# Hybrid block on one core: background steps twice per weight chunk, scores and transposes of p apart

## The chip, the cores and the metric

The kernel runs on one core of one Trainium2 chip. The metric is the device time of one execution in microseconds, median of three runs. The engines have in-order programs of their own: PE (TensorE matmuls and transposes), DVE (VectorE), ACT (ScalarE), POOL (GpSimd) and SP (SyncE, which issues the loads of weights). Accumulators lie in PSUM, everything else in SBUF.

## The reference

One layer on 512 tokens of 1024 features, all in float32. Between two feed-forward parts stands the mixed part, which the change touches:

```
h = rmsnorm(x);  xr, gr, q, k, v, ga, gb = split(h @ w_in)
xc = conv4(xr)                                  # centred, depthwise
a = exp(-8 * r * softplus(-lam));  bx = sqrt(1 - a*a) * (i * xc)   # r, i = sigmoid(gates(xc))
y_lru = (scan_fwd(a, bx) + scan_bwd(a, bx)) * gelu(gr)
q, k = rmsnorm per head of q, k                 # 16 heads of 64
p = softmax(q k^T + bias, over a window of 8 rows x 32 columns)
y_att = p @ v
x = x + (sigmoid(ga) * y_lru + sigmoid(gb) * y_att) @ w_out
```

## The kernel before

Every large product is made in three matmuls of split operands (wh xh + wh xl + wl xh; L147 to L149, and L704 to L706 for q, k, v). A weight chunk is one load of 128 x 1024 floats on SP, one rounding to wh on ACT (L120) and one subtraction to wl on DVE (L123), then 24 matmuls of 512 columns on PE. Three buffers take the raw weights, four each wh and wl. PSUM has four slots named acc and four named aux.

While PE works through the chunks, two background lanes are mixed in. Each is a list of generators: `lru(fs)` for four blocks of the recurrence at a time, and `heads(hf, ...)` for one half of the attention heads (eight of sixteen). `weave(rate)` (L488) adds the rate to what a lane is owed and runs it from one `yield` to the next while a whole step is owed. It is called once behind each chunk. RATE gives the steps per chunk for the phases: xr (the eight chunks of the recurrence's input), t0 (q, k and v of half 0), t1 (q, k, v of half 1) and g (the three gates). Each half's attention is appended when its v group is done, so half 0 runs in t1 and half 1 in g.

The steps of the LRU: gates on PE, ACT and DVE; then per block and direction one exp with a combination (L659), one square root with a product (L664), one scan (L670 forward, L672 backward, with the sum L673).

The steps of attention: rq from the sums of squares (L754 to L756; the sums are L719, the copies out of PSUM L717); the products of q and k with rq (L761); then `start` makes the transposes of q and k for two heads (L770, L772) and splits them (ACT L776, L778, DVE L777 ql, L779 kl); `scores` has 12 matmuls (L796) into two slots, each read by DVE with bias and running maximum (L807, so and nmx), exponentiated on ACT (L810) and normalised on DVE (L812, L816); `turn` transposes p on PE (L824) and copies it out (L827, PT); `apply` multiplies with v (L836) and copies att out (L846). In half 0 a unit is two of four column blocks of a pair of heads, in half 1 all four, with the second pair of slots from acc.

The order of each engine's program is made by a scheduler that respects dependences and priorities, evictions and splits being marked as high priority. So an instruction issued in a step can move ahead of what was written earlier. `after(i, prev)` sets an edge that keeps one instruction behind another in the order on its engine and adds no wait between engines.

Of the kernel before, what the change touches and what calls it, by code (L numbers as in the profile page):

```python
# [16 lines left out]
P = 128  # L17
T = 512
D = 1024
KT = D // P  # L20
# [38 lines left out]
ATT_LAG = (1, 2), (1, 2)  # L59

RATE = {
    "xr": {"lru": 4, "att": 0.0},
    "t0": {"lru": 3, "att": 0.0},
    "t1": {"lru": 2, "att": 0.75},
    "g": {"lru": 3, "att": 0.85},
}


# [1 line left out]
def block_kernel(ctx: ExitStack, tc, a, out):  # L70
# [8 lines left out]
    dram = ctx.enter_context(tc.tile_pool(name="dram", bufs=1, space=bass.MemoryType.DRAM))  # L79

    uid = [0]

    def nm(s):
        uid[0] += 1
# [61 lines left out]
    def mm3(ps, wh, wl, xh, xl, first, last, skip=False):  # L146
        nc.tensor.matmul(ps, wh, xh, start=first, stop=False, skip_group_check=skip)  # L147
        nc.tensor.matmul(ps, wh, xl, start=False, stop=False, skip_group_check=skip)  # L148
        nc.tensor.matmul(ps, wl, xh, start=False, stop=last, skip_group_check=skip)  # L149

    def feat_chunk(src, nk, xh, xl, ps, k0, ktot, act=True):
        H, L = load_w(src, nk * P, act)
        for k in range(nk):
            s = slice(k * P, (k + 1) * P)
            kk = k0 + k
            mm3(ps, H[:, s], L[:, s], xh[kk], xl[kk], kk == 0, kk == ktot - 1)


    def make_xg(gcol, tag):
# [46 lines left out]
    def after(i, prev):  # L206
# [2 lines left out]
        tc.add_manual_dep(i, prev.name, mybir.DependencyInfo(  # L209
            mybir.DependencyClass.NoSync, mybir.DependencyReason.DATA), reason="order")  # L210


    mark = {}

    def sub(out_, in0, in1, neg=False):

# [462 lines left out]
    rb = None  # L679
    for f in range(KT):  # L680
        ps = acc_t()
        feat_chunk(a["wxr"][f], KT, xh, xl, ps, 0, KT)
        if f == 0:
            rb, rcol, vx = rstd(ssum)
            epsv = const.tile([P, NCB], F32, name="epsv")
            nc.vector.tensor_scalar(epsv, vx, EPS, None, ALU.mult)
        conv(f, ps, rb)
        weave(RATE["xr"])
        if (f + 1) % LRU_F == 0:
            lanes["lru"].append(lru(range(f + 1 - LRU_F, f + 1)))  # L690
# [4 lines left out]
    def tok_group(w, hf):  # L695
        pss = [acc_t() for _ in range(NCB)]
        for kp in range(4):
            H, L = load_w(a["wqkv"][w * 2 + hf, kp], 1024)
            for j in range(NCB):
                tj = slice(j * P, (j + 1) * P)  # L700
                for k in range(2):
                    kk = kp * 2 + k
                    s = slice(k * T, (k + 1) * T)
                    nc.tensor.matmul(pss[j], xh[kk][:, tj], H[:, s], start=kk == 0, stop=False)  # L704
                    nc.tensor.matmul(pss[j], xl[kk][:, tj], H[:, s], start=False, stop=False)  # L705
                    nc.tensor.matmul(pss[j], xh[kk][:, tj], L[:, s], start=False, stop=kk == KT - 1)  # L706
            if kp < 3:
                weave(RATE[phase[0]])
        return pss
# [39 lines left out]
    def heads(hf, raws, st):  # L749

        rq = tiny.tile([P, 2, NCB, 8], F32, tag="rq", name=nm("rq"))
        for w in range(2):
            for j in range(NCB):
                nc.vector.tensor_scalar(rq[:, w, j, :], st[:, w, j, :], 1.0 / HD, epsv[:, j : j + 1], ALU.mult, ALU.add)  # L754
        nc.scalar.activation(rq, rq, AF.Sqrt)
        nc.vector.reciprocal(rq, rq)  # L756
        yield
        for w in range(2):
            for j in range(NCB):
                t = raws[w][j].rearrange("p (h d) -> p h d", d=HD)  # L760
                nc.vector.tensor_tensor(t, t, rq[:, w, j, :].unsqueeze(2).to_broadcast([P, 8, HD]), ALU.mult)  # L761
            yield
        qk, rss, soft, PTs = {}, {}, {}, {}

# [1 line left out]
        def start(fi):  # L766
            fs = slice(fi * P, (fi + 1) * P)
            pq, pk = aux_t(), aux_t()
            for j in range(NCB):
                nc.tensor.transpose(pq[:, j * P : (j + 1) * P], raws[0][j][:, fs], ident)  # L770
            for j in range(NCB):
                nc.tensor.transpose(perm(pk)[:, j], raws[1][j][:, fs], ident)  # L772
            rev = lambda t: t.rearrange("p (j t) -> p j t", j=NCB)[:, :, ::-1]
            fwd = lambda t: t.rearrange("p (j t) -> p j t", j=NCB)
            qh, ql, kh, kl = (big_t(F32R, n=n) for n in ("qh", "ql", "kh", "kl"))
            nc.scalar.activation(rev(qh), fwd(pq), AF.Copy, scale=gq8)  # L776
            nc.vector.scalar_tensor_tensor(rev(ql), fwd(pq), gq8, rev(qh.bitcast(F32)), ALU.mult, ALU.subtract)  # L777
            nc.scalar.activation(kh, pk, AF.Copy, scale=gk)  # L778
            nc.vector.scalar_tensor_tensor(kl, pk, gk, kh.bitcast(F32), ALU.mult, ALU.subtract)  # L779
            grid = lambda t: t.rearrange("p (r c) -> p r c", r=ROWS)  # L780
            qk[fi] = qh, ql, grid(kh), grid(kl)

        def scores(fi, n2s):

            qh, ql, kh, kl = qk[fi]
            if 0 in n2s:
                rss[fi] = tiny.tile([P, 2, NCB], F32, tag="rs", name=nm("rs"))
            rs = rss[fi]
            pss = {n2: [aux_t() if n2 == n2s[0] else acc_t() for _ in range(2)] for n2 in n2s}
            for n in [n2 * 2 + i for n2 in n2s for i in range(2)]:  # L790
                ps, i = pss[n // 2], n % 2
                keys = lambda t: t[:, :, KSTART[n] : KSTART[n] + 2 * QC].rearrange("p r (h c) -> p h r c", h=2)
                for q_, k_ in ((qh, kl), (qh, kh), (ql, kh)):
                    for hp in (1, 0):
                        o = slice(hp * HD, (hp + 1) * HD)
                        mm = nc.tensor.matmul(ps[hp][:, i * 256 : (i + 1) * 256], q_[o, n * P : (n + 1) * P], keys(k_[o]),  # L796
                                         start=k_ is kl, stop=q_ is ql)
            for n2, hp in [(n2, hp) for n2 in n2s for hp in range(2)]:
                ps = pss[n2]
                bm = bms[hf * 4 + fi, hp]  # L800
                pt = big_t(n="p")
                so = big_t(n="so")
                nmx = tiny.tile([P, 2], F32, tag="nmx", bufs=4, name=nm("nmx"))
                for i in range(2):
                    n = n2 * 2 + i
                    cs = slice(i * 256, (i + 1) * 256)
                    nc.vector.tensor_tensor_reduce(  # L807
                        so[:, cs], ps[hp][:, cs], bm[:, BTYPE[n]],
                        -1.0, 3.0e38, ALU.add, ALU.min, nmx[:, i : i + 1])
                    nc.scalar.activation(pt[:, cs], so[:, cs], AF.Exp, scale=-1.0, bias=nmx[:, i : i + 1],  # L810
                                         accum_out=rs[:, hp, n : n + 1])
                nc.vector.reciprocal(rs[:, hp, n2 * 2 : n2 * 2 + 2], rs[:, hp, n2 * 2 : n2 * 2 + 2])  # L812
                for i in range(2):
                    n = n2 * 2 + i
                    cs = slice(i * 256, (i + 1) * 256)
                    nc.vector.tensor_scalar(pt[:, cs], pt[:, cs], rs[:, hp, n : n + 1], None, ALU.mult)  # L816
                soft[fi, n2, hp] = pt
            return mm

        def turn(fi, n2, hp):  # L820
            pt = soft.pop((fi, n2, hp))
            pT = aux_t()
            for q in range(4):
                nc.tensor.transpose(pT[:, q * P : (q + 1) * P], pt[:, q * P : (q + 1) * P], ident)  # L824
            PT = big_t(n="PT")
            with tc.high_priority():
                nc.scalar.activation(PT, pT, AF.Copy)  # L827
            PTs[fi, n2, hp] = PT
# [27 lines left out]
        for i in range(len(units) + LC):  # L856
            if i < len(units):
                fi, n2s = units[i]
                last = scores(fi, n2s)
                if i >= LC and 1 in units[i - LC][1]:  # L860
                    apply(units[i - LC][0], last)
                if 0 in n2s:
                    if fi < 3:
                        start(fi + 1)
                    if hf * 4 + fi + 1 < KT:
                        bias(hf * 4 + fi + 1)
            for n2 in (0, 1):
                if 0 <= i - LB < len(units) and n2 in units[i - LB][1]:
                    for hp in range(2):
                        turn(units[i - LB][0], n2, hp)  # L870
                if hf == 1 and n2 == 0:
                    yield
            if len(units) <= i < len(units) + LC and 1 in units[i - LC][1]:
                apply(units[i - LC][0])
            yield
# [12 lines left out]
    def gates(w, fs, fn, scale=1.0):  # L888
        q = [pair_t() for _ in range((len(fs) + 1) // 2)]
        for i, f in enumerate(fs):  # L890
            ps = acc_t()
            feat_chunk(a["wg3"][w * KT + f], KT, xh, xl, ps, 0, KT, f % 2 == 0)
            with tc.high_priority():
                nc.vector.tensor_tensor(q[i // 2][:, i % 2], ps, rb, ALU.mult)
            weave(RATE[phase[0]])
# [131 lines left out]
```

## Time and profile before

| | |
|---|---|
| median of three runs | 1130.19 us (1130.04 to 1130.41) |
| the profiled execution | 1130.12 us |
| its span | 1128.3 us |
| PE, DVE, ACT busy | 1120.5, 837.4, 594.0 us |
| chain that ended last | PE 96%, ACT 1%, DVE 1%, issue 1% |

PE's matmuls are pipelined, so that a busy PE says little of how fast it goes; the distance between the starts of neighbours is what one costs. The span is from the first to the last instruction; 1.8 us of the time lie around it. Idle time of DVE or ACT matters only where PE waits for what comes behind it. A mean over the whole span mixes stages with different limits, so the stretches around the start of attention are shown apart below.

### The profile page before, as it was taken

Reading aid. Unit: us, or ns where it says so; the run is one execution under the profiler, and the core shown is the slowest. Engines: PE = TensorE matmul, PEld = TensorE weight load, DVE = VectorE, ACT = ScalarE, POOL = GpSimd, SP = SyncE. Lnnn points to the kernel's source line nnn. Section 1 sums busy time; section 2 is a strip of 40 time slices with the busy share of each in tenths; the row PEclk is TensorE's granted clock in tenths of the full one; section 3 lists DMA queues with packets and bytes.
Section 4 is the critical chain, followed back from the end, with each engine's and each line's share of the span. In section 5 each row is a group of like instructions: output and inputs, shape, how many; then the busy total and the mean of one; then the engine's idle time right before and its main releaser. Section 6 shows DMA issues by size and latency. Waiting matters only on the chain.

```text
span 1128.3 us, 17240 instructions
## 1 busy us (share of the span) xinstructions
PE 1120.5 (99%) x6867; PEld 992.7 (88%) x6867; DVE 837.4 (74%) x1294; ACT 594.0 (53%) x896; POOL 19.2 (2%) x52
## 2 busy tenths in 40 slices
PE   9999999999999999999999999999999999999998
PEld 7899999988888888888788888888999999998887
DVE  7888888894736798797865687658688888894552
ACT  8554554563624595985564255546445445464340
POOL 0000000000000000010110000000000000000000
PEclk9999999999999999999999999999999999999999
DMA  8242332443433342353453242255133333253421
GB/s 265 92 131 76 117 108 95 135 138 102 131 94 112 94 159 84 113 162 101 135 154 93 94 126 72 88 193 187 56 92 117 92 112 113 91 170 95 131 75 38
DMA packets 43697, 130.69 MB, mean 116 GB/s; under 512 B 5984, under 2 KB 8544, under 8 KB 43616
## 3 DMA queue, kind: packets, MB, share of 16 engines
q1 hardware_dynamic: 39744, 119.36, 34.1%
q0 software_dynamic: 3296, 9.97, 3.0%
q8 instruction: 54, 0.88, 0.3%
q10 hardware_dynamic: 576, 0.26, 0.1%
q14 instruction: 27, 0.22, 0.1%
HBM read 121.17 MB, written 8.39 MB: 115 GB/s over the span
## 4 chain that ended last, share of the span: by engine, by line
PE 96%; ACT 1%; DVE 1%; issue 1%; DMA 0%; ACTq 0%; DVEq 0%
PE acc L267 29%; PE acc L147 11%; PE acc L149 11%; PE acc L148 11%; PE aux L267 5%; PE aux L147 4%; PE aux L148 4%; PE aux L149 4%; PE acc L705 4%; PE acc L704 4%; PE acc L706 3%; PE aux L824 1%; PE aux L836 1%; PE aux L796 1%; PE acc L380 1%
## 5 line engine op out<-in xcount | busy, mean ns | idle before, releaser
L120 ACT ACTIVATE wh<-wraw 128x1024 fp32r<-128x1024 f32 (+3 forms) x242 | 241.2, 999 | 336.8 <-PE acc L148 95.9
L123 DVE TENSOR_TENSOR wl<-wraw,wh 128x1024 fp32r<-128x1024 f32 (+3 forms) x254 | 291.2, 1150 | 139.2 <-ACT wh L120 138.6
L267 PE MATMUL acc<-s,wh 128*128 128x256 f32 x1216 | 220.5, 283 | 0.0
L267 PEld LDWEIGHTS acc<-s,wh 128*128 128x128 f32 x1216 | 189.7, 192 | 0.0
L267 PE MATMUL acc<-s,wl 128*128 128x256 f32 x608 | 172.1, 283 | 0.0
L147 PE MATMUL acc<-xh,wh 128*128 128x512 f32 x304 | 120.1, 395 | 0.0
L149 PE MATMUL acc<-xh,wl 128*128 128x512 f32 x304 | 119.0, 391 | 0.0
L148 PE MATMUL acc<-xl,wh 128*128 128x512 f32 x304 | 118.7, 391 | 0.0
L267 PEld LDWEIGHTS acc<-s,wl 128*128 128x128 f32 x608 | 116.7, 192 | 0.0
L267 PE MATMUL acc<-xh,wl 128*128 128x256 f32 x304 | 86.0, 283 | 0.0
L267 PE MATMUL acc<-xl,wh 128*128 128x256 f32 x304 | 86.0, 283 | 0.0
L267 PE MATMUL acc<-xh,wh 128*128 128x256 f32 x304 | 86.0, 283 | 0.0
L704 PE MATMUL acc<-wh,xh 128*128 128x512 f32 x192 | 75.2, 392 | 0.0
L705 PE MATMUL acc<-wh,xl 128*128 128x512 f32 x192 | 74.8, 390 | 0.0
L706 PE MATMUL acc<-wl,xh 128*128 128x512 f32 x192 | 74.7, 389 | 0.0
L301 DVE TENSOR_TENSOR wraw<-wraw,pair 128x1024 f32<-128x1024 f32 x57 | 69.5, 1220 | 0.8
L147 PE MATMUL aux<-hh,wh 128*128 128x512 f32 (+1 forms) x181 | 69.9, 386 | 0.0
L148 PE MATMUL aux<-hl,wh 128*128 128x512 f32 (+1 forms) x181 | 69.9, 386 | 0.0
L149 PE MATMUL aux<-hh,wl 128*128 128x512 f32 (+1 forms) x181 | 69.9, 386 | 0.0
L149 PE MATMUL acc<-hh,wl 128*128 128x512 f32 (+1 forms) x176 | 67.9, 386 | 0.0
L148 PE MATMUL acc<-hl,wh 128*128 128x512 f32 (+1 forms) x176 | 67.9, 386 | 0.0
L147 PE MATMUL acc<-hh,wh 128*128 128x512 f32 (+1 forms) x176 | 67.9, 386 | 0.0
(210 smaller groups left out, 2195.8 us busy)
## 6 DMA issues: line engine op xcount, KB each, us to landing
wraw<-wqkv SPq DMA_DIRECT2D x24, 512.0 KB, 3.7
wraw<-wg SPq DMA_DIRECT2D x24, 512.0 KB, 3.6
wraw<-w1d SPq DMA_DIRECT2D x22, 512.0 KB, 3.6
wraw<-w2d SPq DMA_DIRECT2D x22, 512.0 KB, 3.6
pair<-w2s SPq DMA_DIRECT2D x20, 512.0 KB, 3.6
wraw<-w2s SPq DMA_DIRECT2D x20, 512.0 KB, 3.6
wraw<-w1s SPq DMA_DIRECT2D x18, 512.0 KB, 3.7
pair<-w1s SPq DMA_DIRECT2D x18, 512.0 KB, 3.6
```

Source lines behind the costliest of these rows:

```text
L120: nc.scalar.activation(H, raw, AF.Copy)
L123: nc.vector.tensor_tensor(L, raw, H.bitcast(F32), ALU.subtract)
L147: nc.tensor.matmul(ps, wh, xh, start=first, stop=False, skip_group_check=skip)
L148: nc.tensor.matmul(ps, wh, xl, start=False, stop=False, skip_group_check=skip)
L149: nc.tensor.matmul(ps, wl, xh, start=False, stop=last, skip_group_check=skip)
L267: nc.tensor.matmul(o, w_[:, c], x_, start=first and m + k == 0 and w_ is H and x_ is xh_, stop=m + k == 4 and w_ is L, skip_group_check=True)
L301: nc.vector.tensor_tensor(t, t, o, ALU.add)
L380: nc.tensor.matmul(pre[i], w[i][1][:, s], xh[k], start=k == 0, stop=False)
L704: nc.tensor.matmul(pss[j], xh[kk][:, tj], H[:, s], start=kk == 0, stop=False)
L705: nc.tensor.matmul(pss[j], xl[kk][:, tj], H[:, s], start=False, stop=False)
L706: nc.tensor.matmul(pss[j], xh[kk][:, tj], L[:, s], start=False, stop=kk == KT - 1)
L796: mm = nc.tensor.matmul(ps[hp][:, i * 256 : (i + 1) * 256], q_[o, n * P : (n + 1) * P], keys(k_[o]), start=k_ is kl, stop=q_ is ql)
```

## The change

RATE is halved for the LRU, and `weave` runs twice per chunk: in the middle of `feat_chunk` (by its new argument `mid`) and behind the second token block in `tok_group`. Attention's rate per call stays 0.75 in t1 and becomes 0.65 in g. `scores` and `turn` get steps of their own, and each `turn` of a unit one. `hold(i)` ties an instruction with the edge of `after` to `mark["mm"]`, the last chunk matmul issued so far: the L754 products, the Sqrt, the L761 products, the transposes of q and k, the scores and the transposes of p.

```diff
 RATE = {
-    "xr": {"lru": 4, "att": 0.0},
-    "t0": {"lru": 3, "att": 0.0},
-    "t1": {"lru": 2, "att": 0.75},
-    "g": {"lru": 3, "att": 0.85},
+    "xr": {"lru": 2, "att": 0.0},
+    "t0": {"lru": 1.5, "att": 0.0},
+    "t1": {"lru": 1, "att": 0.75},
+    "g": {"lru": 1.5, "att": 0.65},
 }
...
-    def feat_chunk(src, nk, xh, xl, ps, k0, ktot, act=True):
+    def feat_chunk(src, nk, xh, xl, ps, k0, ktot, act=True, mid=None):
...
+            if mid is not None and k == nk // 2 - 1:
+                weave(mid)
...
+    def hold(i):
+
+        after(i, mark["mm"])
+        return i
...
+                if j == 1:
+                    weave(RATE[phase[0]])
             if kp < 3:
                 weave(RATE[phase[0]])
...
-                nc.vector.tensor_tensor(t, t, rq[:, w, j, :].unsqueeze(2).to_broadcast([P, 8, HD]), ALU.mult)
+                hold(nc.vector.tensor_tensor(t, t, rq[:, w, j, :].unsqueeze(2).to_broadcast([P, 8, HD]), ALU.mult))
...
-            for n2 in (0, 1):
-                if 0 <= i - LB < len(units) and n2 in units[i - LB][1]:
+            yield
+            if 0 <= i - LB < len(units):
+                for k, n2 in enumerate(units[i - LB][1]):
+                    if k:
+                        yield
                     for hp in range(2):
                         turn(units[i - LB][0], n2, hp)
-                if hf == 1 and n2 == 0:
-                    yield
             if len(units) <= i < len(units) + LC and 1 in units[i - LC][1]:
                 apply(units[i - LC][0])
             yield
```

Lines of the kernel after are 3 to 14 higher than those of before: L123 becomes L126, L704 to L706 L713 to L715, L754 L765, L761 L773, L796 L808, L807 L820, L824 L837.

DVE before, where the LRU's scans end and the first scores are read. The scans' outputs are named th, the split weights wl, the first two transposed heads ql and kl, the first scores so_5145.

```order
L672 SCALAR_TENSOR_TENSOR th_4768<-gate_4759,gate_4765 128x512
L123 TENSOR_TENSOR wl_5188<-wraw_5186,wh_5187 128x1024 [waits DMAHW0_49,PE_49,Activation_49]
L719 TENSOR_REDUCE st_4826<-sq_4994 128x8 [waits Activation_49]
L673 TENSOR_TENSOR th_4753<-th_4753,th_4768 128x512 [waits DVE_49]
L754 TENSOR_SCALAR rq_6134<-st_4826,epsv 128x8 x3
L754 TENSOR_SCALAR rq_6134<-st_4826,epsv 128x8 [waits DVE_49]
L123 TENSOR_TENSOR wl_5293<-wraw_5291,wh_5292 128x1024 [waits DMAHW1_49,PE_49,Activation_49]
L123 TENSOR_TENSOR wl_5326<-wraw_5324,wh_5325 128x1024 [waits DMAHW2_49,PE_49,Activation_49]
L777 SCALAR_TENSOR_TENSOR ql_5089<-aux_5078,gq_3677,qh_5088 128x4x128 [waits Activation_49]
L779 SCALAR_TENSOR_TENSOR kl_5091<-aux_5079,small,kh_5090 128x512 [waits Activation_49]
L123 TENSOR_TENSOR wl_5430<-wraw_5428,wh_5429 128x1024 [waits DMAHW3_49,PE_49,Activation_49]
L807 ISA so_5145,nmx_5146<-aux_5130,bm_4187 128x256 [waits DMASW0_49,PE_49]
```

DVE after, at the last scan of the same blocks. The scores so_5134 read in the last row are the second pair.

```order
L679 SCALAR_TENSOR_TENSOR th_4675<-gate_4666,gate_4672 128x512
L730 TENSOR_REDUCE st_4826<-sq_5060 128x8 [waits Activation_49]
L681 SCALAR_TENSOR_TENSOR th_4702<-gate_4693,gate_4699 128x512
L730 TENSOR_REDUCE st_4826<-sq_5065 128x8 [waits Activation_49]
L682 TENSOR_TENSOR th_4675<-th_4675,th_4702 128x512 [waits DVE_49]
L730 TENSOR_REDUCE st_4826<-sq_5070 128x8 [waits Activation_49]
L679 SCALAR_TENSOR_TENSOR th_4741<-gate_4732,gate_4738 128x512
L730 TENSOR_REDUCE st_4826<-sq_5075 128x8 [waits Activation_49]
L681 SCALAR_TENSOR_TENSOR th_4768<-gate_4759,gate_4765 128x512
L682 TENSOR_TENSOR th_4741<-th_4741,th_4768 128x512 [waits DVE_49]
L126 TENSOR_TENSOR wl_5431<-wraw_5429,wh_5430 128x1024 [waits DMAHW1_49,PE_49,Activation_49]
L820 ISA so_5134,nmx_5135<-aux_5119,bm_4187 128x256 [waits PE_49]
```

Before, all eight scans stand ahead of the first read of scores; now the last four of them stand between the first two pairs and the second two reads of scores.

DVE after, somewhat earlier, at the products of q and k with rq (qk) that are held.

```order
L668 SCALAR_TENSOR_TENSOR gate_4738<-gate_4732,gate_4738 128x512 [waits DVE_49,Activation_49]
L765 TENSOR_SCALAR rq_4865<-st_4191,epsv 128x8 x8
L668 SCALAR_TENSOR_TENSOR gate_4765<-gate_4759,gate_4765 128x512 [waits DVE_49,Activation_49]
L126 TENSOR_TENSOR wl_5087<-wraw_5085,wh_5086 128x1024 [waits DMAHW5_49,PE_49,Activation_49]
L768 RECIPROCAL rq_4865<-rq_4865 128x64 [waits Activation_49]
L673 TENSOR_TENSOR gate_4508<-gate_4508,th_4511 128x512
L773 TENSOR_TENSOR qk_4336<-qk_4336,rq_4865 128x512 [waits DVE_49]
L773 TENSOR_TENSOR qk_4341<-qk_4341,rq_4865 128x512
```

Before, the products stood among the splits ahead of the v copies; now they stand behind all eight of the LRU's combinations (L668) and the first of its square-root products (L673).

PE before, at the end of the chunk ahead of the first scores (aux_5131, aux_5130).

```order
L704 MATMUL acc_5009<-wh_5097,xh_3098 128x512
L705 MATMUL acc_5009<-wh_5097,xl_3099 128x512
L706 MATMUL acc_5009<-wl_5098,xh_3098 128x512
L796 MATMUL aux_5131<-kl_5091,qh_5088 128x256 [waits DVE_49]
L796 MATMUL aux_5130<-kl_5091,qh_5088 128x256
L796 MATMUL aux_5131<-kh_5090,qh_5088 128x256 [waits Activation_49]
```

PE after, at the third pair of scores (aux_5203, aux_5202).

```order
L713 MATMUL acc_5084<-wh_5154,xh_3094 128x512
L714 MATMUL acc_5084<-wh_5154,xl_3095 128x512
L715 MATMUL acc_5084<-wl_5155,xh_3094 128x512
L808 MATMUL aux_5203<-kl_5038,qh_5035 128x256 [waits DVE_49]
L808 MATMUL aux_5202<-kl_5038,qh_5035 128x256 [waits DVE_49]
L808 MATMUL aux_5203<-kh_5037,qh_5035 128x256
```

The chunk that ends ahead of the first pair before is the fourth of its group (acc_5009); after, the third pair already follows the second chunk of the group whose slots are acc_5081 to acc_5084, and both of its slots wait for DVE.

## Rows read from the trace of the kernel before

**Rows 1.** The page: busy time, share of the span and instructions of each engine.

```profile
PE 1120.5 (99%) x6867; PEld 992.7 (88%) x6867; DVE 837.4 (74%) x1294; ACT 594.0 (53%) x896; POOL 19.2 (2%) x52
```

**Rows 2.** Timeline of PE, 27 matmuls apart: start, duration, line, operands.

```profile
482.66 0.39 PE L706 MATMUL acc<-wl,xh 128*128 128x512 f32 x1
...
488.78 0.39 PE L706 MATMUL acc<-wl,xh 128*128 128x512 f32 x1
```

**Rows 3.** Waits of PE: us in total, times, longest.

```profile
PE aux L824 <- ACT att L846: 1.2, 1, 1.2
...
PE aux L824 <- DVE nmx L807: 0.8, 2, 0.6
```

**Rows 4.** Timeline of PE at three transposes of p; idle before in brackets.

```profile
546.80 0.39 PE L704 MATMUL acc<-wh,xh 128*128 128x512 f32 x1
547.77 0.66 PE L824 MATMUL aux<-ident,p 128*128 128x128 f32 x4 [0.58 <-DVE nmx L807]
...
665.63 0.60 PE L772 MATMUL aux<-ident,qk 128*128 128x128 f32 x4
666.49 1.01 PE L824 MATMUL aux<-ident,p 128*128 128x128 f32 x5 [0.25 <-DVE nmx L807]
...
684.72 0.40 PE L148 MATMUL acc<-xl,wh 128*128 128x512 f32 x1
686.33 0.66 PE L824 MATMUL aux<-ident,p 128*128 128x128 f32 x4 [1.22 <-ACT att L846]
```

**Rows 5.** Windows: PE, PEld, DVE, ACT, POOL busy, then PEclk, DMA, GB/s.

```profile
480.60:516.50 35.90, 35.90 (x160) 29.73 (x159) 35.37 (x48) 24.34 (x35) 4.28 (x7) 1.00 0.52 150
516.50:545.00 28.50, 28.50 (x162) 23.33 (x160) 19.00 (x50) 20.07 (x38) 1.14 (x2) 1.00 0.40 123
```

**Rows 6.** Groups of DVE from 480.6 to 546: busy us, mean ns, idle before.

```profile
L123 DVE TENSOR_TENSOR wl<-wraw,wh 128x1024 fp32r<-128x1024 f32 x12 | 14.6, 1216 | 9.7 <-ACT wh L120 9.7
...
L664 DVE TENSOR_TENSOR gate<-gate,th 128x512 f32<-128x512 f32 x8 | 5.1, 684 | 0.5 <-ACT th L662 0.5
...
L672 DVE TENSOR_TENSOR_SCAN th<-gate,gate 128x512 f32<-128x512 f32 x4 | 4.9, 1214 | 0.0
...
L728 DVE TENSOR_SCALAR v<-acc,rcol 128x512 f32<-128x512 f32 x4 | 2.9, 747 | 0.0
...
L816 DVE TENSOR_SCALAR p<-p,rs 128x256 f32<-128x256 f32 x8 | 2.5, 349 | 0.1
```

**Rows 7.** Timeline of DVE: last v copy, neighbours, small products, reads of scores.

```profile
485.63 0.74 DVE L728 TENSOR_SCALAR v<-acc,rcol 128x512 f32<-128x512 f32 x1
...
508.47 1.20 DVE L670 TENSOR_TENSOR_SCAN th<-gate,gate 128x512 f32<-128x512 f32 x1
509.58 0.66 DVE L719 TENSOR_REDUCE st<-sq 128x8 f32<-128x512 f32 x1
...
514.79 0.62 DVE L754 TENSOR_SCALAR rq<-st,epsv 128x8 f32<-128x8 f32 x4
...
526.11 0.42 DVE L807 CUSTOM_DVE_ANT_0 so<-aux,bm 128x256 f32<-128x256 f32 x1
...
526.45 0.42 DVE L807 CUSTOM_DVE_ANT_0 so<-aux,bm 128x256 f32<-128x256 f32 x1
```

**Rows 8.** Timeline of PE at the first and the third pair of scores.

```profile
523.99 0.38 PE L796 MATMUL aux<-kl,qh 64*128 64x256 f32 x2
...
524.90 0.66 PE L770 MATMUL aux<-ident,qk 128*128 128x128 f32 x4
...
525.75 0.48 PE L704 MATMUL acc<-wh,xh 128*128 128x512 f32 x1
...
544.26 0.38 PE L796 MATMUL aux<-kl,qh 64*128 64x256 f32 x2
```

**Rows 9.** Group of ACT from 516 to 545: the exps.

```profile
L810 ACT ACTIVATE p<-so,nmx 128x256 f32<-128x256 f32 x8 | 4.0, 502 | 0.6 <-DVE nmx L807 0.3 <-DVE rs L812 0.2
```

**Rows 10.** Timeline of PE at its first instructions.

```profile
1.06 3.41 PE L113 MATMUL aux<-ones 128*128 128x128 f32 x16 [1.06 <-DVE pol L578]
```

More of the change, by code (lines that the diff above doesn't have):

```diff
@@ L81, in block_kernel @@
     uid = [0]
+    mark = {}
     def nm(s):
@@ L148, in mm3 @@
         nc.tensor.matmul(ps, wh, xl, start=False, stop=False, skip_group_check=skip)
-        nc.tensor.matmul(ps, wl, xh, start=False, stop=last, skip_group_check=skip)
-    def feat_chunk(src, nk, xh, xl, ps, k0, ktot, act=True):
+        mark["mm"] = nc.tensor.matmul(ps, wl, xh, start=False, stop=last, skip_group_check=skip)
+    def feat_chunk(src, nk, xh, xl, ps, k0, ktot, act=True, mid=None):
         H, L = load_w(src, nk * P, act)
@@ L210, in after @@
             mybir.DependencyClass.NoSync, mybir.DependencyReason.DATA), reason="order")
-    mark = {}
+    def hold(i):
+        after(i, mark["mm"])
+        return i
     def sub(out_, in0, in1, neg=False):
@@ L681, in block_kernel @@
         ps = acc_t()
-        feat_chunk(a["wxr"][f], KT, xh, xl, ps, 0, KT)
+        feat_chunk(a["wxr"][f], KT, xh, xl, ps, 0, KT, mid=RATE["xr"])
         if f == 0:
@@ L705, in tok_group @@
                     nc.tensor.matmul(pss[j], xl[kk][:, tj], H[:, s], start=False, stop=False)
-                    nc.tensor.matmul(pss[j], xh[kk][:, tj], L[:, s], start=False, stop=kk == KT - 1)
+                    mark["mm"] = nc.tensor.matmul(pss[j], xh[kk][:, tj], L[:, s], start=False, stop=kk == KT - 1)
+                if j == 1:
+                    weave(RATE[phase[0]])
             if kp < 3:
@@ L753, in heads @@
             for j in range(NCB):
-                nc.vector.tensor_scalar(rq[:, w, j, :], st[:, w, j, :], 1.0 / HD, epsv[:, j : j + 1], ALU.mult, ALU.add)
-        nc.scalar.activation(rq, rq, AF.Sqrt)
+                hold(nc.vector.tensor_scalar(rq[:, w, j, :], st[:, w, j, :], 1.0 / HD, epsv[:, j : j + 1],
+                                             ALU.mult, ALU.add))
+        hold(nc.scalar.activation(rq, rq, AF.Sqrt))
         nc.vector.reciprocal(rq, rq)
@@ L769, in start @@
             for j in range(NCB):
-                nc.tensor.transpose(pq[:, j * P : (j + 1) * P], raws[0][j][:, fs], ident)
+                hold(nc.tensor.transpose(pq[:, j * P : (j + 1) * P], raws[0][j][:, fs], ident))
             for j in range(NCB):
-                nc.tensor.transpose(perm(pk)[:, j], raws[1][j][:, fs], ident)
+                hold(nc.tensor.transpose(perm(pk)[:, j], raws[1][j][:, fs], ident))
             rev = lambda t: t.rearrange("p (j t) -> p j t", j=NCB)[:, :, ::-1]
@@ L795, in scores @@
                         o = slice(hp * HD, (hp + 1) * HD)
-                        mm = nc.tensor.matmul(ps[hp][:, i * 256 : (i + 1) * 256], q_[o, n * P : (n + 1) * P], keys(k_[o]),
-                                         start=k_ is kl, stop=q_ is ql)
+                        mm = hold(nc.tensor.matmul(
+                            ps[hp][:, i * 256 : (i + 1) * 256], q_[o, n * P : (n + 1) * P], keys(k_[o]),
+                            start=k_ is kl, stop=q_ is ql))
             for n2, hp in [(n2, hp) for n2 in n2s for hp in range(2)]:
@@ L823, in turn @@
             for q in range(4):
-                nc.tensor.transpose(pT[:, q * P : (q + 1) * P], pt[:, q * P : (q + 1) * P], ident)
+                hold(nc.tensor.transpose(pT[:, q * P : (q + 1) * P], pt[:, q * P : (q + 1) * P], ident))
             PT = big_t(n="PT")
@@ L891, in gates @@
             ps = acc_t()
-            feat_chunk(a["wg3"][w * KT + f], KT, xh, xl, ps, 0, KT, f % 2 == 0)
+            feat_chunk(a["wg3"][w * KT + f], KT, xh, xl, ps, 0, KT, f % 2 == 0, RATE[phase[0]])
             with tc.high_priority():
```

## The prediction

> **What bounds the kernel now.** I read the page's table of busy time first: PE is busy for 99% of the span and DVE for 74% [rows 1]. The profiled run took 1130.12 us around a span of 1128.3, against a median of 1130.19, so a sum made against it can be read against the median as it stands. PE executes in order; its time is a chain of start-to-start steps: 27 matmuls of 512 columns take 6.12 us, 0.2267 each, so a weight chunk of 24 takes 5.44 us [rows 2]. The change adds and removes no arithmetic, so it can gain only what PE waits, and lose only by new waits or by how the blocks on PE are cut.
>
> The view of PE's waits says what there is to gain. In the mixed stage it holds two entries, both at the transposes of p: 1.2 us behind the copy of att and 0.8 us behind the reads of the scores [rows 3]. The timeline has the places: after a matmul at 684.72 the transposes start at 686.33, 1.61 us later instead of 0.23; after one at 546.80 they start at 547.77, 0.97 instead of 0.23 [rows 4]. That is 1.38 + 0.74 = 2.1 us. At a third place the next transposes start 0.86 us after the first of four, at 665.63, which by the spacing below would take 0.42; with a delay of 0.2 inside the later four it comes to some 0.6. So the most to be won is 2.75 us, 0.24% of the time.
>
> Then I asked what the helpers do there. From 480.6 to 516.5 DVE is busy for 35.37 of 35.90 us; from 516.5 to 545.0 for 19.00 of 28.50 [rows 5]. DVE's 74% is a mean over these two: full while the LRU scans end, and then slack. In the kernel before attention's first scores stand in the slack half.
>
> **The change part by part.**
>
> *Rates.* LRU gets half the rate twice as often: nothing. In phase t1 attention keeps 0.75 but is called twice per chunk, 1.5 steps instead of 0.75. In g it gets 1.3 instead of 0.85, with one step more per unit. So half 0's attention runs about twice as fast through its steps, from the end of the v group on. Counted in the order of PE, its first q/k transposes come 3 chunks after that group instead of 6, the three first pairs of scores 3.6, 5 and 6 chunks after it instead of 7, 8 and 10. Before, from the last v copy, at 485.63, to the third pair, at 544.26 [rows 7, 8], there were 58.6 us.
>
> *Hold.* The eight multiplications by rq (L761), the eight L754 and the Sqrt may no longer move ahead of the chunk issued last. The order of DVE shows the effect: before, they were done between splits ahead of the last v copies; now they stand behind them, among the LRU's L659 and L664. What is late next is the list that DVE has to work off.
>
> *That list.* From the last v copy to the last read of the second pair of scores DVE executes, in order and without a place to rest: 32 operations of 512 columns or priced so (7 L659, 8 L664, 8 L761, 4 L673, 4 L719, the reciprocal L756), 6 splits L123, 8 scans, 1 v copy, 4 of ql and kl, 8 small L754, 8 reads of scores L807, 4 products L816 and 2 reciprocals L812. The third pair of scores needs the slots of PSUM that the last four reads free. Durations [rows 6, 7]: a 512-column operation 0.684 (the row of L664; the other lines have the same shape), a split 1.216, a scan 1.214, a copy of v 0.747, a product 0.349. Two neighbours overlap: a scan at 508.47 lasts 1.20 but the next operation starts 1.11 later, so 0.09 comes off each. Four L754 last 0.62, 0.135 apart; reads of scores follow 0.34 apart. Sum: 32 x 0.594 = 19.0; 6 x 1.126 = 6.8; 8 x 1.12 = 9.0; v, ql, kl 5 x 0.657 = 3.3 (ql and kl priced as v); L754 1.1; reads 2.7; six small 6 x 0.26 = 1.6. Together 43.5 us.
>
> *PE over the same piece.* 6 chunks, 144 x 0.2267 = 32.6; 24 transposes of 128 columns; two pairs of scores. Scores from 523.99 to the transposes at 524.90 are 0.91, eight transposes from there to 525.75 are 0.85, 0.106 each [rows 8]. So 32.6 + 2.5 + 1.8, and 0.3 for switches between kinds: 37.3 us. DVE is the longer by 43.5 - 37.3 = 6.2 us, and PE has to wait that long by the third pair of scores, wherever in the piece it does so. I expect it in two parts: about 4 us ahead of a q or k chunk whose PSUM banks wait for ACT's copies L717, which stand behind the exps of the scores (eight exps take 4.0 us of ACT, [rows 9]), and 2 us at the third pair itself. Before, the same list had 58.6 us and was no bound.
>
> Bounds of this term. Counted only from the end of the first scores, DVE's remainder is 21.3 us by the same durations and PE's 15.8 to 16.2: at least 5.1. If the 4 us behind ACT do not lie in the same time but come on top, at most 10.4. And if DVE's order at run time left it no longer than PE, 0. I take 6.2, since it rests on counted rows.
>
> *Separate steps for scores and transposes.* Turns now come half a chunk or more (2.7 us) behind their scores, more than the 1.61 that the longest gap took. Both waits go, -2.75 (bound: -2.0 by the view of waits). What is late next: the q/k transposes after the third pair wait for the copies PT, which stand behind four exps of 0.50 each [rows 9]; by spacing about 0.6. In phase g a whole unit is now scored half a chunk earlier against its ql and kl: 0.2 to 0.3 of waiting.
>
> *Cut of the blocks.* PE's blocks of attention go from 95 to 111. A switch between matmuls, scores and transposes costs 0.01 to 0.15 (the difference in start gaps where kinds meet, over the spacing within a kind). Sixteen more, partly replacing dearer ones: +0.4.
>
> Sum: 1130.1 - 2.75 + 6.2 + 0.6 + 0.3 + 0.4 = 1134.9, so 1135.
>
> The page "Perfetto Trace Analysis" of the Trainium skill, section "Optimization Strategy", says that where the most-contended engine changes between regimes, interleaving the regimes may help. That would favour this change, which spreads attention over more chunks' halves; but [rows 5] has DVE, not PE, as the engine without slack in the first regime, and the change draws attention into that regime instead of out of it. By the rule the sum would end at the first rival's time; by the rows, above before.
>
> **Rivals.**
>
> *A: the list is hidden and only the waits go.* -2.75 + 0.4 leaves 1127.8, faster. For it: DVE has a quarter of its time free [rows 1]. It decides if DVE's list is shorter than 37.3 us, by 14%; against it stands that every item is counted and [rows 5] shows the same mix of work filling DVE.
>
> *B: waits change places.* DVE catches up so that 2.5 to 3 us of new waiting replace the old: 1130 to 1131. For it: some of the list's items may be worked off while PE does the v group; against it: all 35.9 us there are already full.
>
> *C: PE's clock.* The granted clock is 1.00 in both stretches [rows 5], the 2.4 GHz level, through the idle 1.22 of [rows 4]; no stretch of this trace has an idle of 4 us, so none shows what follows one. At the start, after 1.06 us without work, 16 matmuls of 128 columns take 3.41 us, 0.213 each, twice the 0.106 of the transposes [rows 10]. If a wait of 4 us brings that back, the time lost is of that size, 3.41 - 1.7 = 1.7: 1135 + 1.7, about 1137.
> The Trainium skill's page "TensorE: Matmul & The Clock Gate", section "Why this matters for your kernels", warns of such drops behind idle gaps between bursts. That would give C's time; the trace has no gap that tests it.
>
> *D: the eviction wait adds to the wait at the scores*, 10.4 instead of 6.2: about 1139.
>
> **How the numbers follow.** Forecast 0.48, at 1133.3 to 1136.3; A 0.10, B 0.15, C 0.16, D 0.09; 0.02 for the rest. A measurement of this kernel tells 0.2% (2.3 us) from no change: faster is below 1127.9, slower above 1132.5. A is on the line of faster and same, B is same, forecast, C and D are slower: faster 0.09, same 0.17, slower 0.74. The range leaves out A and the upper end of D: 1130.0 to 1139.0.
>
> **What would show it.** In the profile after, PE's waits should lose both entries at the transposes of p and get entries in the first 40 us after the v group: some 4 us at a q or k chunk's first matmul behind ACT's L717 copy (by its new number), and 1 to 2 us at the third pair of scores behind DVE's read of scores. DVE should be without idle time from the last v copy to that pair, in 43 to 44 us. PE's path outside this piece should be the same within 1 us. Wrong would be: DVE idle between the v copies and the third pair (A or B), a granted clock under 1 behind the wait (C), or waits in phase g of over 1 us, which I have not priced.

## The result and the profile after

The kernel after takes 1135.3 us (1134.63 to 1135.67, six runs) against 1130.18 for the kernel before, a ratio of 1.0043 with a 95% interval of 1.0033 to 1.0054. It is slower by 5.1 us, 0.3 off the forecast of 1135.0. The way there is only partly the one forecast.

The page of the kernel after, and its view of cores, to be read against [rows 1]: PE is busy for 2 us longer, in a span that is 5.3 us longer.

```profile
PE 1122.5 (99%) x6867; PEld 994.7 (88%) x6867; DVE 836.1 (74%) x1294; ACT 586.6 (52%) x890; POOL 19.3 (2%) x52
```

```profile
core 0: 1133.6 us, clock 0.997
```

PE's waits after, against [rows 3]. Both entries at the transposes of p are gone; one new entry is there, and none at the third pair of scores.

```profile
PE acc L713 <- ACT qk L728: 5.3, 1, 5.3
PE aux L116 <- DVE pol L587: 1.1, 1, 1.1
```

The timeline of PE at that place. A chunk's last matmul starts at 508.98; the next group's first one, whose PSUM bank still holds the q group, at 514.70: 5.72 us instead of the 0.23 of [rows 2], so 5.5 are lost.

```profile
502.90 0.39 PE L715 MATMUL acc<-wl,xh 128*128 128x512 f32 x1
...
508.98 0.39 PE L715 MATMUL acc<-wl,xh 128*128 128x512 f32 x1
514.70 0.79 PE L713 MATMUL acc<-wh,xh 128*128 128x512 f32 x1 [5.33 <-ACT qk L728]
515.29 0.63 PE L714 MATMUL acc<-wh,xl 128*128 128x512 f32 x1
515.72 0.63 PE L715 MATMUL acc<-wl,xh 128*128 128x512 f32 x1
...
519.13 0.58 PE L714 MATMUL acc<-wh,xl 128*128 128x512 f32 x1
519.55 0.40 PE L715 MATMUL acc<-wl,xh 128*128 128x512 f32 x1
...
530.07 0.38 PE L808 MATMUL aux<-kl,qh 64*128 64x256 f32 x2
```

Behind the wait the matmuls are 0.43 us apart instead of 0.23. The 11 steps from 514.70 to 519.55 take 4.85 us; at the old spacing they take 2.49, so 2.4 us are lost here. The windows (columns as in [rows 5]) show why: the granted clock is 0.50, the level of 1.2 GHz, from 514.7 to 519.5. They also show DVE without idle time up to 519.5.

```profile
484.76:508.90 24.14, 24.14 (x123) 19.97 (x122) 24.11 (x45) 14.09 (x23) 2.67 (x5) 1.00 0.58 172
508.90:514.70 5.80, 0.47 (x4) 0.04 (x2) 5.80 (x11) 5.75 (x14) 0.00 (x0) 0.83 0.00 0
514.70:519.50 4.80, 4.80 (x11) 3.79 (x12) 4.80 (x11) 3.01 (x6) 0.00 (x0) 0.50 0.29 109
519.50:530.10 10.60, 10.60 (x60) 8.33 (x58) 10.23 (x23) 4.95 (x13) 1.13 (x2) 1.00 0.22 64
```

DVE after, its first and last rows of the list that the prediction counted: last v copy, first read of scores, a scan, and the fourth read of the second pair.

```profile
484.76 0.75 DVE L739 TENSOR_SCALAR v<-acc,rcol 128x512 f32<-128x512 f32 x1
...
506.72 0.42 DVE L820 CUSTOM_DVE_ANT_0 so<-aux,bm 128x256 f32<-128x256 f32 x1
...
507.41 1.22 DVE L679 TENSOR_TENSOR_SCAN th<-gate,gate 128x512 f32<-128x512 f32 x1
...
527.74 0.42 DVE L820 CUSTOM_DVE_ANT_0 so<-aux,bm 128x256 f32<-128x256 f32 x1
```

From 484.76 to 528.08, where the next read would start, it is 43.3 us; 43.5 were counted. But the third pair of scores starts at 530.07, two microseconds after the list's end: DVE is not what it waits for. What the 5.3 us wait for stands in ACT's timeline.

```profile
502.38 0.68 ACT L790 ACTIVATE kh<-aux,small 128x512 fp32r<-128x512 f32 x1
508.70 1.28 ACT L823 ACT_TABLE_LOAD   x1 [5.64 <-DVE th L679]
510.00 0.51 ACT L823 ACTIVATE p<-so,nmx 128x256 f32<-128x256 f32 x1
...
513.50 0.67 ACT L790 ACTIVATE kh<-aux,small 128x512 fp32r<-128x512 f32 x1
514.07 0.58 ACT L728 ACTIVATE qk<-acc 128x512 f32<-128x512 f32 x1
```

ACT stands idle for 5.64 us with the first exps (L823) at the head of its program. By the profile the scan th (L679) releases it: the read of 506.72 is done long before. Then come a table load, four exps, a weight chunk's rounding and the two copies of the next heads, and only at 514.07 the copy (L728) that empties the q group's first bank. That bank's last matmul is the sixth of the chunk, at 502.90, so the bank has been complete since 503.3: its copy could have run in nearly the whole of ACT's idle time (with 0.70 in t1, below, it starts as soon as that matmul ends, at 503.83), but it stood behind the exps in ACT's order. The first scores now fall into the middle of the q group's last chunk, so their exps were issued ahead of the copies.

The account, by rows: -2.75 (old waits) + 5.5 + 2.4 = 5.1 us; the spans differ by 5.3. For sums as fine as this the stage is better taken between two marks: the first matmul behind half 0's v group, and the first one on yh, which begins the product with w_out. Before, then after:

```profile
484.93 0.39 PE L704 MATMUL acc<-wh,xh 128*128 128x512 f32 x1
...
736.77 0.50 PE L147 MATMUL acc<-yh,wh 128*128 128x512 f32 x1
```

```profile
484.56 0.39 PE L713 MATMUL acc<-wh,xh 128*128 128x512 f32 x1
...
741.91 0.39 PE L150 MATMUL acc<-yh,wh 128*128 128x512 f32 x1
```

That is 251.84 and 257.35 us, 5.5 more, which leaves 0.4 for the cuts of the blocks. The first mark itself moves from profile to profile: the kernel with filler below, the same as after up to there, has it at 485.18.

### The profile page after: what moved, and what is told of

It reads as the page before. It is cut to its first block, busy times and chain, and to the rows that moved or that the text cites. A ratio compares the mean times of both kernels' runs of the same rounds, so it can differ in the third digit from the quotient of the medians.

```text
span 1133.6 us, 17227 instructions
## 1 busy us (share of the span) xinstructions
PE 1122.5 (99%) x6867; PEld 994.7 (88%) x6867; DVE 836.1 (74%) x1294; ACT 586.6 (52%) x890; POOL 19.3 (2%) x52
## 4 chain that ended last, share of the span: by engine, by line
PE 98%; DVE 1%; ACT 1%; DMA 0%; issue 0%; ACTq 0%
PE acc L276 29%; PE acc L150 11%; PE acc L151 11%; PE acc L152 11%; PE aux L276 5%; PE aux L151 4%; PE aux L152 4%; PE aux L150 4%; PE acc L713 4%; PE acc L714 4%; PE acc L715 4%; PE aux L849 1%; PE aux L837 1%; PE aux L808 1%; PE acc L389 1%; PE aux L389 0%
## 5 line engine op out<-in xcount | busy, mean ns | idle before, releaser
L123 ACT ACTIVATE wh<-wraw 128x1024 fp32r<-128x1024 f32 (+3 forms) x242 | 241.3, 999 | 322.3 <-PE acc L276 95.9
L126 DVE TENSOR_TENSOR wl<-wraw,wh 128x1024 fp32r<-128x1024 f32 (+3 forms) x254 | 291.3, 1151 | 143.3 <-ACT wh L123 142.6
L713 PE MATMUL acc<-wh,xh 128*128 128x512 f32 x192 | 77.0, 401 | 5.3 <-ACT qk L728 5.3
L715 PE MATMUL acc<-wl,xh 128*128 128x512 f32 x192 | 75.7, 394 | 0.0
```

What stands on the lines that cost most here:

```text
L123: nc.scalar.activation(H, raw, AF.Copy)
L126: nc.vector.tensor_tensor(L, raw, H.bitcast(F32), ALU.subtract)
L715: mark["mm"] = nc.tensor.matmul(pss[j], xh[kk][:, tj], L[:, s], start=False, stop=kk == KT - 1)
```

## The experiments

Two theories were set against each other. Theory A, the forecast's: PE waits for the length of DVE's list. Theory B: it waits for the order on ACT, copies behind exps, and the list only sets when the exps run. Each ratio is against the kernel before on the same chip.

### The q and k products freed

```diff
-                hold(nc.vector.tensor_tensor(t, t, rq[...], ALU.mult))
+                nc.vector.tensor_tensor(t, t, rq[...], ALU.mult)
```

and the same for L765 and the Sqrt.

> The kernel after, with hold() taken off the eight rq products, the Sqrt and the eight products of q and k with rq; all other holds, rates and steps stay. Theory A (the length of DVE's list is what PE waits for): DVE's list behind the last v copy loses 8 x 0.594 + 1.1 + 0.55 = 6.4 us, 37 us against PE's 37.3, so the wait of 5.3 us goes and with it the low clock: about 1128. Theory B (the order on ACT: the copies of the finished q group out of PSUM stand behind the first exps, and the exps behind whatever DVE has ahead of the first reads of scores): in this kernel's order the exps still stand ahead of the copies, and DVE has seven scans ahead of the first read, which by durations puts that read at about 511 instead of 506.7; the wait stays or grows, 5 to 7 us in one or two pieces: 1135 to 1137.

Measured: 1138.66 us (1137.4 to 1138.74), ratio 1.0072 [1.0057, 1.0087], slower than after. PE's waits, then DVE at its first read of scores and ahead of the second pair's reads:

```profile
PE acc L713 <- ACT qk L728: 6.0, 1, 6.0
PE aux L807 <- DVE kl L790: 2.2, 1, 2.2
```

```profile
511.12 0.41 DVE L819 CUSTOM_DVE_ANT_0 so<-aux,bm 128x256 f32<-128x256 f32 x1
...
526.93 1.23 DVE L126 TENSOR_TENSOR wl<-wraw,wh 128x1024 fp32r<-128x1024 f32 x1 [4.28 <-ACT wh L123]
```

A shorter list made the wait longer, as B said. In the kernel after all eight scans come behind the first read of scores (506.72, the first scan at 507.41), and not only the last four; here all eight come ahead of it, and it starts at 511.12. hold() on these products was no cause; it kept scans behind the reads. Theory A in its plain form falls here: DVE even stands idle for 4.28 us ahead of the second pair's reads, and PE waits all the same. B had the direction and missed the size: the two waits are 8.2 us where 5 to 7 stood, and the time is 1.7 us above its range.

### Only the reads and exps of the first scores half a chunk later

```diff
+            if (hf, fi, n2s) == (0, 0, (0,)):
+                later.append(reads)     # run behind the step's yield
+            else:
+                reads()
```

> The kernel after with the very first scores' matmuls where they are on PE (3.6 chunks behind the v group), but their reads on DVE and exps on ACT issued one step, half a chunk, later; number of steps, rates and holds stay. In ACT's order the copies of the q group now stand ahead of the exps. Theory A (the wait is owed to the early scores and DVE's list as such): the list up to the third pair is no shorter, so 4 to 6 us of waiting remain somewhere: 1133 to 1136. Theory B (the order on ACT): the 5.3 us at the k group's first matmul fall to 1 or less and the clock stays at 1.00; the copies are still late by up to 1 us for the second slot and the transposes of p by 1 us behind the later reads: 1130 to 1132.

Measured: 1131.16 us (1130.78 to 1131.69), ratio 1.0008 [0.9998, 1.0018]. PE's waits, and two windows: from the last v copy to the k group's first matmul, and on to 530.00; then DVE's last read of the second pair and PE's start of the third:

```profile
PE aux L843 <- DVE p L831: 1.4, 1, 1.4
PE acc L713 <- ACT qk L728: 1.1, 2, 0.7
```

```profile
484.85:509.80 24.95, 24.60 (x124) 20.00 (x122) 24.92 (x43) 15.89 (x26) 2.67 (x5) 1.00 0.56 166
509.80:530.00 20.20, 18.10 (x99) 13.74 (x100) 20.20 (x47) 14.10 (x30) 1.14 (x2) 1.00 0.32 92
```

```profile
524.33 0.40 DVE L822 CUSTOM_DVE_ANT_0 so<-aux,bm 128x256 f32<-128x256 f32 x1
```

```profile
525.81 0.39 PE L809 MATMUL aux<-kl,qh 64*128 64x256 f32 x2
```

The first scores' matmuls stand where they did after (505.14, 505.06), DVE is as full, and the 5.3 us are 1.1 in two pieces, with the clock at 1.00, as B said; the time is 4.1 us less than after. But reads and exps moved together, and the list did not stay as long as was expected: from 484.85 the fourth read of the second pair ends the list at 524.66, after 39.8 us and not 43.3, since two scans and two sums now stand behind it. By its length alone Theory A would ask for 39.8 - 37.3 = 2.5 us, and PE loses some 2.9 by spacing. What speaks for B is the place: the third pair starts 1.1 us behind the list's end and waits for nothing. How much of the 4.1 us belongs to ACT's order by itself is not shown.

### One call moved behind the q group

```diff
-                if j == 1:
+                if j == 1 and not (hf == 1 and w == 0 and kp == 3):
                     weave(RATE[phase[0]])
...
         weave(RATE[phase[0]])
+        if hf == 1 and w == 0:
+            weave(RATE[phase[0]])
```

> The kernel after, with one call moved: in the last chunk of the first q group in phase t1 the step in the middle of the chunk runs behind the group instead. The first scores then come behind the chunk and the copies out of PSUM stand ahead of the exps in ACT's order; holds, rates and the number of steps stay. Theory A: the list in front of the third pair of scores loses only three scans and two sums, and is 38 to 39 us against PE's 37.3: a wait of 1 to 1.5 us at the scores at least, up to the old 5 if what was moved behind is late too: 1129 to 1133. Theory B: no wait at the chunk, clock at 1.00 throughout: 1127.5 to 1129.

Measured: 1130.79 us (1130.6 to 1131.32), ratio 1.0006 [0.9996, 1.0015]. No wait behind L728, clock 0.999, but:

```profile
PE aux L839 <- DVE ql L791: 1.5, 1, 1.5
...
PE aux L810 <- DVE nmx L822: 0.5, 2, 0.3
```

B's place was right and its price too low; the time lies in A's range. With the order mended, DVE's list, 38.6 us here, shows up after all, with some 3 us by spacing (0.97 at the second pair, 2.2 at the transposes of p). Theory A is the second bound, not the first.

### One number: 0.70 instead of 0.75

```diff
-    "t1": {"lru": 1, "att": 0.75},
+    "t1": {"lru": 1, "att": 0.70},
```

> The kernel after with one number changed: attention's rate in t1 is 0.70 per call instead of 0.75. The first scores come at chunk 4.0 behind the v group instead of 3.6, the third pair at 6.5 instead of 6; holds, separate steps and cuts stay, and in ACT's order the copies of the q group out of PSUM now stand ahead of the exps. Theory A (the length of DVE's list): some 40 us of DVE stand against 40 of PE up to the third pair, so a part of the 5.5 us stays, 0 to 2 us: 1128 to 1131. Theory B (the order on ACT): no wait at that chunk, clock at 1.00: 1127.3 to 1128.3, all of the loss and the two old waits at the transposes gone. A rival for both, that the cuts and holds cost more than 0.4 us in themselves: over 1130 without a wait in the view of waits.

Measured: 1128.49 us (1128.11 to 1128.97), ratio 0.9983 [0.9975, 0.9992]: faster than before. PE's only wait in the mixed stage, a window of it, and ACT:

```profile
PE aux L837 <- DVE kl L791: 0.5, 1, 0.5
```

```profile
508.00:524.00 16.00, 15.54 (x92) 12.68 (x91) 16.00 (x38) 11.25 (x25) 0.30 (x1) 1.00 0.23 67
```

```profile
503.83 0.60 ACT L728 ACTIVATE qk<-acc 128x512 f32<-128x512 f32 x1 [0.26 <-PE acc L715]
...
511.52 0.58 ACT L728 ACTIVATE qk<-acc 128x512 f32<-128x512 f32 x1
...
514.55 0.51 ACT L823 ACTIVATE p<-so,nmx 128x256 f32<-128x256 f32 x1
```

The time is 0.2 us above B's range and inside A's. All four copies stand before the first exp, the last from 511.52 to 512.10. DVE is busy for 16.00 of 16.00 us, exactly as full as after, and PE waits for 0.5 us, at the transposes of p: a full DVE is no bound where what PE needs comes early in its order. For A stands that the list is shorter than was expected: from 485.26 to the end of the fourth read of the second pair, at 523.90, it takes 38.6 us and not 40, with three scans behind it, and PE takes 40.8 to the third pair. So A too allows for no wait there, and this kernel alone does not tell the two apart. Holds, separate steps and cuts are those of after. So they cost little: between the marks the stage takes 250.13 us, 1.7 less than before, which is -2.75 + 0.6 (this wait by spacing) + 0.4 for the rest; the medians differ by 1.85.

### Filler in the gap

```diff
+        if (w, hf) == (1, 1):
+            for n in (17, 1):
+                fill = aux_t()
+                for _ in range(n):
+                    hold(nc.tensor.matmul(fill, xh[0][:, :P], xh[0], start=True, stop=True))
         pss = [acc_t() for _ in range(NCB)]
```

> The kernel after, with 18 matmuls of 512 columns into two unused PSUM tiles set into the idle time ahead of the k group of half 1 (18 x 0.2267 = 4.1 us of the 5.3). They compute nothing that is used. If the low clock of 0.50 behind the wait comes from the idle time, it stays at 1.00 and 11 matmuls save 0.20 each: 2.2 us less than after, about 1133.1. If it comes from something else, no change, or slower by what the filler delays: 1135 to 1136.

Measured: 1134.47 us (1134.31 to 1134.84), ratio 1.0038 [1.0023, 1.0053]. The clock held, but between the marks the stage takes 256.18 us, so that 1.2 us came back and not 2.2. (The medians are 0.8 us apart, a difference that the intervals of the two ratios do not set apart from zero.)

```profile
PE acc L718 <- ACT qk L733: 2.0, 2, 1.3
```

```profile
509.00:515.30 6.30, 5.08 (x23) 3.87 (x21) 6.30 (x12) 5.94 (x13) 0.00 (x0) 1.00 0.00 0
515.30:521.00 5.70, 4.89 (x20) 3.75 (x21) 5.70 (x12) 3.87 (x7) 0.00 (x0) 1.00 0.30 93
```

```profile
515.34 0.50 PE L718 MATMUL acc<-wh,xh 128*128 128x512 f32 x1 [1.26 <-ACT qk L733]
...
519.35 0.39 PE L720 MATMUL acc<-wl,xh 128*128 128x512 f32 x1
520.50 0.50 PE L718 MATMUL acc<-wh,xh 128*128 128x512 f32 x1 [0.77 <-ACT qk L733]
```

The idle time is what lowers the clock here. But the copies of the later banks (L733 is L728 in this kernel) come at their own pace: a faster PE meets them at 520.50, 0.9 us late by spacing. The group begins as late behind the first mark as after (30.16 us, 30.14). 2.4 - 0.9 leaves 1.5, of which the marks show 1.2; the rest is not accounted for. The low clock after lay partly over a wait that would have been there anyway.

### The early start alone, in the kernel before

```diff
         nc.vector.reciprocal(rq, rq)
-        yield
+        if hf == 1:
+            yield
...
-            yield
+            if hf == 1 or w == 1:
+                yield
```

> The kernel before with two of the three pauses ahead of the first q/k transposes taken out for half 0: its first scores come 4 chunks behind the v group instead of 7; no holds, no separate steps, one call per chunk, rate 0.75. In its order the q group's copies stand ahead of the exps and the products with rq ahead of the v copies. If the early start alone made the loss (DVE full of LRU work): 1133 to 1136. Theory B: no wait behind the copies; the transposes of p wait as before, in some more places (0.5 to 1.5 us each): 1130 to 1132.

Measured: 1131.82 us (1131.61 to 1132.16), ratio 1.0013 [1.0004, 1.0022], as B said: no wait behind the copies, and the old waits in more places.

```profile
PE aux L826 <- ACT att L848: 1.2, 1, 1.2
PE aux L826 <- DVE nmx L809: 1.2, 4, 0.5
```

Attention that starts three chunks sooner costs 1.5 us here, not 5.

### The start put off by four empty steps

```diff
+        for _ in range(4 if hf == 0 else 0):
+            yield
```

> The kernel after, with four empty steps ahead of half 0's attention: its first scores come 6 chunks behind the v group instead of 3.6, the third pair 9; holds, rates and separate steps stay. Both theories: PE has 54 us up to the third pair, DVE's list of 43 us is hidden, the q group's copies come ahead of the exps: no wait of over 1 us, clock 1.00; the two old waits at the transposes of p are gone as well: 1127.5 to 1129, below before. If holds and cuts themselves cost more than I priced (0.4 us): 1130 to 1133.

Measured: 1132.76 us (1132.59 to 1134.66), ratio 1.0027 [1.0017, 1.0036]: a miss of both theories. New waits came elsewhere:

```profile
PE aux L786 <- DVE qk L775: 1.7, 2, 1.4
PE acc L150 <- DVE v L739: 1.4, 1, 1.4
```

```profile
517.00:519.00 2.00, 0.59 (x3) 0.35 (x2) 2.00 (x4) 0.07 (x1) 0.00 (x0) 0.89 0.34 31
519.00:522.00 3.00, 3.00 (x9) 2.35 (x9) 3.00 (x5) 0.69 (x1) 0.00 (x0) 0.51 0.41 157
```

The first: the held products of q and k are now tied to a later chunk and come behind more of the LRU, so the q/k transposes wait for them, and the clock falls to 0.51 behind it. The second comes where the next phase begins, at a late copy of v; what made it late was not tested. The profile is not that of the median: of the ten executions six take 1132.59 to 1132.78 us at a mean granted clock of 1.000, and four, the profiled one (1134.27) among them, 1134.24 to 1134.66 at 0.998. So the fall of the clock costs some 1.6 us and comes in four of ten; the other 2.4 us over before are there without it. A later start is thus no cure in itself.

### A version faster than both

With 0.70 in t1 and 0.55 in g:

> The kernel after with 0.70 instead of 0.75 in t1 and 0.55 instead of 0.65 in g. Theory B: as with 0.70 alone, 1127.3 to 1128.3; the slower rate in g should change little, since the kernel after shows no wait there: within 0.5 us of it.

Measured: 1127.99 us (1127.84 to 1128.21), ratio 0.9978 [0.9969, 0.9987]. It is faster than before, and within 0.5 us of 0.70 alone, as expected.

## Why the prediction was right in size and half right in cause

- *Old waits, -2.75.* Right: both entries are gone.
- *DVE's list, 43.5 us.* Measured 43.3 us with hardly any idle time.
- *"PE has to wait that long by the third pair of scores, wherever in the piece it does so."* This is the step that failed. It took the end of the list as the bound. PE was bound earlier, by the copy L728 behind the exps, for 5.5 us where "about 4" stood; with that wait and the low clock behind it, the third pair came 2.0 us after the list's end and waited for nothing, where 2 us stood. The place on ACT was named, but taken as part of DVE's account. That the list's length is not what PE waits for there is shown by the freed products (list shorter, wait longer). The reads half a chunk later (wait 1.1) show that the place can be mended, though with a list of 39.8 us and not 43.3.
- *+0.6 behind PT, +0.3 in g.* Neither is there. *Cuts, +0.4*: 0.4 is left between the marks, after and at 0.70. The count behind it is not what the traces show: there the stretches of attention between chunk matmuls go from 27 to 32 in this stage, not up by sixteen.
- *Rival C, the clock.* Taken at 0.16 and 1.7 us on its own; it happened, by one of the prediction's own signs of being wrong, with 2.4 us by spacing, of which 1.2 came back with the filler. The page "TensorE: Matmul & The Clock Gate" of the Trainium skill, section "Why this matters for your kernels", was the right warning: the trace after has 0.50 behind an idle 5.33 us.
- The total was near by luck. The 2 us at the third pair and the 0.9 of PT and g did not come; in their place came 1.3 more at the copy (5.5 for the 4.2 that 6.2 leaves) and 2.4 of low clock.
- *Rival A* was not far: 0.05 less in one rate gives 1128.5, where A said 1127.8, with the list shorter than PE's time, which was A's condition.
- One reading was not right, and moves nothing in the sum: [rows 5] has PE as full as DVE in the first stretch (35.90 and 35.37 of 35.90 us), not DVE alone.

What stays open: that the first exps waited for the scan because the buffer of p had been the scan's operand is read from the order of releases; no kernel was run that takes this wait away alone. Nor was one run that moves the copies ahead of the exps on ACT and leaves DVE's order as it is, so B's price by itself stays open.

## What to carry to other kernels

Where background work is woven in at a finer grain, look at what each step is issued ahead of: a step that falls just before the end of an accumulation group puts its own ACT work ahead of the copies that free the group's banks, and the next group pays. A list of work that is as long as PE's stretch is a warning, not a price; here the price was set by the first thing in an in-order program that PE needed, and by what stood ahead of it. After a wait of some microseconds look at the granted clock too, and do not book the whole of it as a loss, since other waits lie under it.

## What was not expected of the hardware

The granted clock did not follow the length of the last wait alone. It fell to 0.50 behind 5.33 us without a matmul, to 0.51 behind 6.00 in the kernel with freed products, and to 0.51 in the kernel with the late start behind waits of 0.28 and 1.41 us with single transposes between them (PE busy for 0.59 of 2.00 us), and that in four of its ten executions only. It stayed at 1.00 behind 2.22 us in the kernel with freed products (at its first scores), behind 1.4 in the one with late reads, and behind 1.22 before [rows 4].
